# Five up blocks as seven products of quarters' sums, in a hybrid layer on one core

## The chip, the core and the metric

One Trainium2 chip, one of its cores. The metric is the device time of one execution in microseconds, from its start to its end; the median of the runs is quoted, and beside it one execution that the hardware profiler recorded. The engines have short names in the profile: PE is TensorE's matmuls, PEld its weight loads, DVE is VectorE, ACT is ScalarE, POOL is GpSimd, SP is SyncE, which issues most of the DMAs.

## What is computed

One layer over 512 tokens of width 1024 in float32. An mLSTM and a sparse attention with compressed, selected and window branches share one input product; their outputs go through `w_out`; then comes the feed-forward part with a causal convolution of width 3 on the gate, and a gated embedding with a last norm:

```python
x = x + jnp.concatenate([m_out, a_out], axis=-1) @ w_out[i]
x = x + conv_ffn(rms_norm(x, ln2_g[i]), w_up[i], conv_w[i], conv_b[i], w_down[i])
gate = jax.nn.sigmoid(rms_norm(x, ple_norm_g[i]) @ w_ple_gate[i])
x = x + gate * (p[i].astype(x.dtype) @ w_ple_proj[i])
return rms_norm(x, final_g)

def conv_ffn(h, w_up, conv_w, conv_b, w_down):
    u = h @ w_up                                # 1024 -> 2 * 2048
    gate, val = jnp.split(u, 2, axis=-1)
    gate = lax.conv_general_dilated(gate, conv_w[:, None, :], ...) + conv_b
    return (jax.nn.silu(gate) * val) @ w_down   # 2048 -> 1024
```

## The kernel before

Features lie on the partitions and tokens along the free axis, so a product takes a block of 128 x 128 weights as the stationary operand and 512 tokens as the moving one. Every float32 operand is split into a high part, rounded to the type fp32r, and a low part, the rest; a product is then three matmuls per block of the contraction: high x high, high x low, low x high. The function `gemm` (L445) sends the 16 matmuls with the high weights first (L449, L450), then the 8 with the low weights (L453).

The weights come as a stream of jobs (`Stream`, L182), each of 512 KB, 128 x 1024 columns: `load` (L152) issues its DMA on SP into one of two rooms `raw`, `split` (L163) makes the high part on ACT (L166) and the low part on DVE (L167), each in one of two rooms. `step` (L214) starts a job's matmuls and splits the job behind it (`prepare(1)`, L221). Other work is hung on the kernel's own count of time with `st.after`. Each engine works through its instructions in an order that is fixed when the program is built; the engines meet at semaphores.

In the feed-forward part the loop of L1203 makes 16 blocks f of two up jobs each: part 0 is the gate's 128 columns and part 1 the value's. `up_job` (L1105) multiplies `x2h` and `x2l`, the split of X x ln2_g without the norm's factor, by the weights. `up_evac` (L1150) takes the sum out of PSUM: for the gate a product with the norm's factor `n2["rb"]` on DVE (L1154), the convolution with one scaled copy on ACT (L1157) and two steps on DVE (L1158, L1159), and silu on ACT (L1160); for the value two products on DVE (L1164, L1165) and its split into `U` (ACT L1167, DVE L1168). POOL only clears the two columns in front of the gate (L1153). The PSUM banks are taken from two pairs in turn (`pW`, L106). The norm's factor comes from `start_norm` (L1123) soon after the first up jobs. Then 16 down jobs follow (`down_job`, L1184), and the last pass, in which the last tile's matmuls have 256 columns (L1333 to L1335).

POOL's other large work lies in the attention, far ahead: the scaling of the exponentials (L810).

Of the kernel before, what the change touches and what calls it, by code (L numbers as in the profile page):

```python
# [15 lines left out]
S = 512  # L16
PE_ORDER = False
D = 1024
KB = 8
# [23 lines left out]
LASTW = 256  # L43
SPLIT = 384
# [29 lines left out]
def hybrid_block_kernel(ctx: ExitStack, tc: tile.TileContext, a, out):  # L74
# [88 lines left out]
    def split(name, raw, shape):  # L163
        hi = wpool.tile(shape, F32R, tag="hi", name=name + "h")
        lo = wpool.tile(shape, F32R, tag="lo", name=name + "l")
# [16 lines left out]
    class Stream:  # L182


        def __init__(self):
            self.jobs, self.loaded, self.ready, self.cur, self.done = [], [], [], None, set()
            self.now, self.events, self.debt = 0.0, [], 0.0

        def add(self, name, src, shape, run):
            self.jobs.append((name, src, shape, run))  # L190

        def load(self, depth):
            while len(self.loaded) < depth and self.jobs:
                name, src, shape, run = self.jobs.pop(0)
                self.loaded.append((name, load(name, src, shape), shape, run))
                if name == "mv3":
                    early[0] = None

        def prepare(self, depth):
            while len(self.ready) < depth and (self.jobs or self.loaded):  # L200
                self.load(1)
                name, raw, shape, run = self.loaded.pop(0)
                self.ready.append((name, run, split(name, raw, shape)))
# [58 lines left out]
    identb = consts.tile([128, 128], BF, name="identb")  # L262
    maskt = consts.tile([128, 128], BF, name="maskt")
# [204 lines left out]
    gz = consts.tile([128, NT, 36], F32, name="gz")  # L468
    sg = consts.tile([128, NT, 24], F32, name="sg")
# [130 lines left out]
    VW = 4 * 132  # L600

    def vones(j, h):
        return vo[:, j * VW + h * 132:j * VW + h * 132 + 130]

# [518 lines left out]
    def start_norm(norm, acc, name):  # L1123
# [9 lines left out]
        def rows(ah, al):  # L1133
# [12 lines left out]
            for fn in norm.get("pending", []):  # L1146
                fn()
        st.after(T_NS, stats)

    def up_evac(f, part, ps, rb2):  # L1150
        if part == 0:
            zg = fpool.tile([128, S + 2], F32, name=f"zg{f}", tag="zg")
            GE.memset(zg[:, 0:2], 0.0)  # L1153
            VE.tensor_mul(zg[:, 2:S + 2], ps, rb2)  # L1154
            cw = lambda j: cols[:, C_CW + 16 * j + f:C_CW + 16 * j + f + 1]
            cv = fpool.tile([128, S], F32, name=f"cv{f}", tag="cv")
            SE.activation(cv, zg[:, 2:S + 2], AF.Identity, scale=cw(2), bias=cols[:, C_CB + f:C_CB + f + 1])  # L1157
            VE.scalar_tensor_tensor(cv, zg[:, 1:S + 1], cw(1), cv, op0=ALU.mult, op1=ALU.add)  # L1158
            VE.scalar_tensor_tensor(cv, zg[:, 0:S], cw(0), cv, op0=ALU.mult, op1=ALU.add)  # L1159
            SE.activation(cv, cv, AF.Silu)  # L1160
            n2["cv"] = cv
        else:
            zv = fpool.tile([128, S], F32, name=f"zv{f}", tag="zv")
            VE.tensor_mul(zv, ps, rb2)  # L1164
# [38 lines left out]
    for f in range(16):  # L1203
        for part in range(2):
# [19 lines left out]
    gF = main.tile([128, 2, 512], F32, tag="mixa", name="gF")  # L1224
# [218 lines left out]
```

## Time and profile before

| | us |
|---|---|
| median of three runs (626.46 to 627.56) | 626.55 |
| the profiled execution | 627.01 |
| its span, from the first to the last instruction | 625.2 |
| PE busy in the span | 613.9 |
| DVE busy | 417.8 |
| ACT busy | 317.8 |
| POOL busy | 62.2 |

The page gives busy time by engine and by 40 equal slices of the span; the other views group instructions by line, list them in order of time, or sum them over a stretch. A matmul's duration in these rows holds its way through the array; how densely matmuls follow each other is read from their starts.

### The profile page before, as it was taken

To read this page: it belongs to the slowest core of one execution; us is meant where nothing else is said; L and a number is where in the kernel's file an instruction comes from. 1 tells how busy PE (TensorE), PEld (TensorE's weight loads), DVE (VectorE), ACT (ScalarE), POOL (GpSimd) and SP (SyncE) were. 2 spreads that over 40 slices of the span, in tenths; PEclk is the share of its full clock that TensorE was granted. 3 is DMA by queue.
4 is the path that set the end of the run, shared out by engine and by line. 5 is a ranking of instruction groups with operands and counts; after the bars stand their busy time and mean duration, and the time that the engine had idled before them with its cause. 6 is when DMAs were issued, how large, how long until landed. Compare 5 with 4: busy or idle time off the path is not lost. (4 is left out here: it accounts for less than half of the span.)

```text
span 625.2 us, 8416 instructions
## 1 busy us (share of the span) xinstructions
PE 613.9 (98%) x3011; PEld 500.0 (80%) x3011; DVE 417.8 (67%) x800; ACT 317.8 (51%) x665; POOL 62.2 (10%) x132
## 2 busy tenths in 40 slices
PE   9999999999999999999999999999999999999994
PEld 7888877777777777888878888888888888888884
DVE  6988857787777878882977565655556434345386
ACT  7456556677667766653745333334334223233254
POOL 0400009332333400000000000000000000000000
PEclk9999999999999999999999999999999999999998
DMA  8812136112221323122233332233333222634703
GB/s 315 297 63 73 34 102 156 48 35 68 68 65 38 110 93 101 35 69 67 95 108 101 102 97 83 91 100 101 102 101 102 94 94 84 166 103 142 195 1 136
DMA packets 23210, 63.04 MB, mean 101 GB/s; under 512 B 2744, under 2 KB 7736, under 8 KB 23100
## 3 DMA queue, kind: packets, MB, share of 16 engines
q1 hardware_dynamic: 21632, 59.93, 29.5%
q0 software_dynamic: 1248, 2.16, 1.5%
q8 instruction: 24, 0.39, 0.3%
q10 hardware_dynamic: 288, 0.41, 0.2%
q14 instruction: 18, 0.15, 0.1%
HBM read 56.72 MB, written 2.10 MB: 94 GB/s over the span
## 5 line engine op out<-in xcount | busy, mean ns | idle before, releaser
L810 POOL TENSOR_SCALAR E<-E,rr,sg 128x512 f32<-128x512 f32 (+3 forms) x54 | 38.0, 704 | 72.0 <-DVE rr L805 57.8
L839 DVE TENSOR_TENSOR pl<-pt,ph 128x512 fp32r<-128x512 f32 x40 | 27.2, 686 | 7.3 <-ACT ph L838 6.9
L1164 DVE TENSOR_TENSOR zv<-pu,n2rb 128x512 f32<-128x512 f32 x16 | 11.0, 690 | 31.1 <-PE pu L453 31.1
L1167 ACT ACTIVATE u<-zv 128x512 fp32r<-128x512 f32 x16 | 10.1, 632 | 42.6 <-DVE zv L1165 42.6
L838 ACT ACTIVATE ph<-pt 128x512 fp32r<-128x512 f32 x40 | 23.7, 599 | 15.4 <-PE pt L835 14.0
L835 PE MATMUL pt<-cols,E 128*128 128x128 f32 x160 | 26.4, 274 | 0.5 <-DVE E L810 0.4
L1154 DVE TENSOR_TENSOR zg<-pu,n2rb 128x512 f32<-128x512 f32 x16 | 11.1, 692 | 22.3 <-PE pu L453 22.3
L1153 POOL MEMSET zg<- 128x2 f32 x16 | 1.5, 100 | 242.2 <-DVE cv L1159 149.7
L835 PEld LDWEIGHTS pt<-cols,E 128*128 128x128 f32 x160 | 19.9, 140 | 6.4 <-DVE E L810 1.1
L1194 DVE TENSOR_TENSOR X<-pd,X 128x512 f32<-128x512 f32 x8 | 5.5, 692 | 29.2 <-PE pd L453 29.2
L1157 ACT ACTIVATE cv<-zg,cols 128x512 f32<-128x512 f32 x16 | 13.1, 817 | 20.8 <-DVE zg L1154 20.8
L1160 ACT ACTIVATE cv<-cv 128x512 f32<-128x512 f32 x16 | 10.1, 632 | 25.8 <-DVE cv L1159 25.8
L803 ACT ACTIVATE E<-s,nm 128x384 f32<-128x384 f32 (+2 forms) x48 | 22.2, 471 | 0.0
L843 PE MATMUL pv<-ph,V 128*128 128x512 f32 x40 | 18.8, 471 | 0.0
L1168 DVE TENSOR_TENSOR u<-zv,u 128x512 fp32r<-128x512 f32 x16 | 11.0, 691 | 9.8 <-ACT u L1167 9.8
L805 DVE RECIPROCAL rr<-rs 128x3 f32<-128x3 f32 x32 | 5.5, 172 | 16.8 <-ACT E L803 16.7
L845 PE MATMUL pv<-pl,V 128*128 128x512 f32 x40 | 16.5, 411 | 0.1
L793 DVE TENSOR_REDUCE nm<-s 128x2 f32<-128x768 f32 (+2 forms) x24 | 16.3, 680 | 0.0
L286 DVE TENSOR_TENSOR acc<-acc,sq 128x512 f32<-128x512 f32 x21 | 14.4, 684 | 0.1
L803 ACT ACTIVATE Ec<-s,nm 128x32 f32<-128x32 f32 x24 | 6.8, 283 | 13.5 <-DVE nm L793 10.5
L1159 DVE SCALAR_TENSOR_TENSOR cv<-zg,cols,cv 128x512 f32<-128x512 f32 x16 | 12.0, 751 | 0.5
L1158 DVE SCALAR_TENSOR_TENSOR cv<-zg,cols,cv 128x512 f32<-128x512 f32 x16 | 11.9, 746 | 0.0
(1219 smaller groups left out, 2023.3 us busy)
## 6 DMA issues: line engine op xcount, KB each, us to landing
X<-in_xg SPq DMA_DIRECT2D x1, 2048.0 KB, 8.7
xo<-xturn SPq DMA_DIRECT2D x32, 64.0 KB, 2.1
wgr<-in_w_pg SPq DMA_DIRECT2D x4, 512.0 KB, 4.0
s1r<-in_w_s SPq DMA_DIRECT2D x3, 676.0 KB, 8.9
xT<-in_xg SPq DMA_DIRECT2D x3, 514.0 KB, 7.9
rawx<-in_w_mv SPq DMA_DIRECT2D x3, 512.0 KB, 6.7
Q<-hlq POOLq DMA_DIRECT2D x12, 128.0 KB, 3.1
out_y<-xo SPq DMA_DIRECT2D x3, 512.0 KB, 2.6
```

The lines of the kernel that those rows point to most:

```text
L286: return VE.tensor_add(acc[:, :n], acc[:, :n], sq[:, :n])
L793: VE.tensor_reduce(out=nm[:, 1:3], in_=sw, axis=AX.X, op=ALU.max, negate=True)
L803: SE.activation(e, p, AF.Exp, bias=nm[:, b:b + 1], accum_out=rs[:, b:b + 1])
L810: eng.tensor_scalar(e, e, rr[:, b:b + 1], sg[:, i, 3 * h + b:3 * h + b + 1], op0=ALU.mult, op1=ALU.mult)
L835: TE.transpose(pt[:, r * 128:(r + 1) * 128], Es[r][:, c0:c0 + 128], ident)
L838: SE.activation(ph, pt, AF.Copy)
L839: VE.tensor_sub(pl, pt, f32(ph))
L843: TE.matmul(pv, vs, ph, start=first, stop=False)
L845: TE.matmul(pv, vs, pl, start=False, stop=last)
L1157: SE.activation(cv, zg[:, 2:S + 2], AF.Identity, scale=cw(2), bias=cols[:, C_CB + f:C_CB + f + 1])
L1158: VE.scalar_tensor_tensor(cv, zg[:, 1:S + 1], cw(1), cv, op0=ALU.mult, op1=ALU.add)
L1159: VE.scalar_tensor_tensor(cv, zg[:, 0:S], cw(0), cv, op0=ALU.mult, op1=ALU.add)
```

## The change

Blocks f = 7 to 11 are computed as a 2 x 2 product of halves with seven products in place of eight. The contraction (8 blocks of 128) is cut in two halves, the tokens in two halves of 256, and the two columns of the product are gate and value. The left factors are quarters of the weights and sums of them, the right ones quarters of the normed input and sums of those. Each product has 4 blocks of contraction, three matmuls each, of 256 columns (`seven`). A block's stream entries are four: the gate's weights (products 1 and 2), the first two weights' sums (6 and 5), the other two (7 and 3; the input of product 3 is a plain quarter), and half of the value's weights (product 4). The value's weights are loaded with the second entry and the last two load nothing; POOL makes the four sums s1 to s4 when that load is entered (`landed_b`), in three rooms of 128 x 1024 columns of which a block takes two. The products stand in halves of four PSUM banks, with the other four for the next block, and are put together by seven additions on DVE and one copy on ACT.

For this the input is scaled by the norm's factor beforehand (`scaled_input`, in eight rounds), split into `xnh` and `xnl`; POOL makes 16 sums of its quarters in `Tf`, which are split in four rounds (`split_sums`). From f = 5 on the ordinary blocks read `xnh` and `xnl` too and lose the factor `rb` in their evacuation: the gate's sum is copied by ACT, the value's has one product on DVE in place of two.

Rooms: `raw`, `hi` and `lo` get a third room while `st.ahead` is set (from f = 6 to f = 11), the stream splits two jobs ahead and loads three. `identb`, `maskt`, `gz` and `sg` move to a pool that ends with the attention, the rows of `vo` become 130 columns a head in place of 132, and the room for descriptors of DMAs issued by POOL becomes 1024 bytes. `U`'s quarters, `xo`, `x3h` and `gF` change places.

```diff
+FAST = (7, 8, 9, 10, 11)
+UNSCALED = 5
+T_XN = 0.4, 5.4
+T_TS = 2.0, 5.4
+AHEAD = 3
...
+    turns = {}
+    def more(tag, n, extra, shape, dt, name):
+        if st.ahead:
+            turns[tag] = (turns.get(tag, -1) + 1) % (n + extra)
+            if turns[tag] >= n:
+                return fpool.tile(shape, dt, tag=tag, bufs=extra, name=name)
+        return wpool.tile(shape, dt, tag=tag, bufs=n, name=name)
...
-            raw = wpool.tile(shape, F32, tag="raw", bufs=2, name=name + "r")
+            raw = more("raw", 2, 1, shape, F32, name + "r")
-        hi = wpool.tile(shape, F32R, tag="hi", name=name + "h")
+        hi = more("hi", 2, 1, shape, F32R, name + "h")
+        lo = more("lo", 2, 1, shape, F32R, name + "l")
...
-                self.prepare(1)
+                self.prepare(self.depth)
+                self.load(self.ahead)
...
-    gz = consts.tile([128, NT, 36], F32, name="gz")
-    sg = consts.tile([128, NT, 24], F32, name="sg")
+    identb = apool.tile([128, 128], BF, name="identb")
+    maskt = apool.tile([128, 128], BF, name="maskt")
+    gz = apool.tile([128, NT, 36], F32, name="gz")
+    sg = apool.tile([128, NT, 24], F32, name="sg")
...
-    VW = 4 * 132
+    VW = 4 * 130
...
+            elif f < UNSCALED:
+                yield from gemm(ps, wh, wl, range(KB), x2h, x2l, range(KB))
             else:
-                yield from gemm(ps, wh, wl, range(KB), x2h, x2l, range(KB))
+                yield from gemm(ps, wh, wl, range(KB), xnh, xnl, range(KB))
+                up_evac(f, part, ps, None)
+                return
...
+            for q, b in enumerate((0, 4, 1, 5, 2, 6, 3, 7)):
+                st.after(T_XN[0] + T_XN[1] * q, lambda b=b: scaled_input(b))
...
+            if rb2 is None:
+                SE.activation(zg[:, 2:S + 2], ps, AF.Copy)
...
+            if rb2 is None:
+                VE.tensor_mul(zv, ps, n2["cv"])
...
+    def scaled_input(b):
+        xn = t2k(f"xn{b}")
+        i = VE.scalar_tensor_tensor(xn, X[:, b], cols[:, C_G2 + b:C_G2 + b + 1], n2["rb"], op0=ALU.mult, op1=ALU.mult)
+        SE.activation(xnh[:, b], xn, AF.Copy)
+        VE.tensor_sub(xnl[:, b], xn, f32(xnh[:, b]))
+        n2["xn", b] = xn
+        if b >= 4:
+            j = b - 4
+            top = n2["xn", j]
+            b11, b12, b21, b22 = top[:, 0:H], top[:, H:], xn[:, 0:H], xn[:, H:]
+            t1, t2, t3, t4 = (Tf[:, j, q] for q in range(4))
+            GE.tensor_sub(t1, b12, b11)
+            GE.tensor_sub(t3, b22, b12)
+            GE.tensor_sub(t2, b22, t1)
+            GE.tensor_sub(t4, b21, t2)
+    def split_sums(j):
+        SE.activation(Th[:, j], Tf[:, j], AF.Copy)
+        VE.tensor_sub(Tl[j // 2][:, j % 2], Tf[:, j], f32(Th[:, j]))
+    def seven(ps, w, x):
+        (wh, wl), (rh, rl) = w, x
+        for j in range(4):
+            TE.matmul(ps, wh[:, j], rh(j), start=j == 0, stop=False)
+            TE.matmul(ps, wh[:, j], rl(j), start=False, stop=False)
+            yield 0.24
+        for j in range(4):
+            TE.matmul(ps, wl[:, j], rh(j), start=False, stop=j == 3)
+            yield 0.12
...
+    def fast_banks(f):
+        fast_turn[0] += 1
+        if fast_turn[0] % 2:
+            ps = [pG(f"pfa{f}"), pT(f"pfb{f}"), pG(f"pfc{f}"), pT(f"pfd{f}")]
+        else:
+            sa = pSa(f"pfa{f}")
+            ps = [sa[:, 0], sa[:, 1], pSb(f"pfc{f}"), pV(f"pfd{f}")]
+        return [p[:, t0:t0 + H] for p in ps for t0 in (0, H)]
...
+        def landed_b(raw):
+            r0, d["r1"] = d["r0"], raw
+            if not rooms:
+                rooms.append(fpool.tile([128, 3, 8, 128], F32, bufs=1, name="ws", tag="xturn"))
+                rooms.append(0)
+            sums = []
+            for _ in range(2):
+                sums.append(rooms[0][:, rooms[1] % 3])
+                rooms[1] += 1
+            s2, s1, s3, s4 = sums[0][:, 0:4], sums[0][:, 4:8], sums[1][:, 0:4], sums[1][:, 4:8]
+            GE.tensor_add(s1, raw[:, 0:4], raw[:, 4:8])
+            GE.tensor_sub(s2, s1, r0[:, 0:4])
+            GE.tensor_sub(s3, r0[:, 0:4], raw[:, 0:4])
+            GE.tensor_sub(s4, r0[:, 4:8], s2)
+            d["sums"] = sums
+        def prep_b(name, raw, shape):
+            return split(name, d["sums"][0], shape)
+        def prep_c(name, raw, shape):
+            return split(name, d["sums"][1], shape)
+        def prep_d(name, raw, shape):
+            return split(name, d["r1"][:, 4:8], shape)
+        def run_a(wh, wl):
+            d["ps"] = fast_banks(f)
+            d["u"] = t2k(f"fu{f}")
+            d["v"] = t2k(f"fv{f}")
+            p1, p2 = d["ps"][0:2]
+            yield from seven(p1, half((wh, wl), 0), quarter(0, 0))
+            v1 = d["v"][:, H:]
+            yield from seven(p2, half((wh, wl), 1), quarter(4, 0))
+            SE.activation(v1, p1, AF.Copy)
+            d["zg"] = gate_rows(f)
+            VE.tensor_add(d["zg"][:, 2:2 + H], p2, v1)
+        def run_b(wh, wl):
+            p1, p2, p6, p5 = d["ps"][0:4]
+            u2, u4 = d["u"][:, 0:H], d["v"][:, 0:H]
+            yield from seven(p6, half((wh, wl), 0), tsum(1))
+            yield from seven(p5, half((wh, wl), 1), tsum(0))
+            VE.tensor_add(u2, p6, d["v"][:, H:])
+            VE.tensor_add(u4, p5, u2)
+        def run_c(wh, wl):
+            p5, p7, p3 = d["ps"][3:6]
+            u2, u3, u4 = d["u"][:, 0:H], d["u"][:, H:], d["v"][:, 0:H]
+            d["zv"] = fpool.tile([128, S], F32, name=f"zv{f}", tag="zv")
+            yield from seven(p7, half((wh, wl), 0), tsum(2))
+            yield from seven(p3, half((wh, wl), 1), quarter(4, H))
+            VE.tensor_add(d["zg"][:, 2 + H:], p3, u4)
+            convolve(f, d["zg"])
+            VE.tensor_add(u3, p7, u2)
+            VE.tensor_add(d["zv"][:, H:], p5, u3)
+        def run_d(wh, wl):
+            zv, p4 = d["zv"], d["ps"][6]
+            yield from seven(p4, (wh, wl), tsum(3))
+            VE.tensor_add(zv[:, 0:H], p4, d["u"][:, H:])
             VE.tensor_mul(zv, zv, n2["cv"])
-            uh, ul = U[f // 4][:, 0, f % 4], U[f // 4][:, 1, f % 4]
-            SE.activation(uh, zv, AF.Copy)
-            VE.tensor_sub(ul, zv, f32(uh))
+            hidden(f, zv)
...
+        st.add(f"wu{f}0", a["w_up"][:, f, 0], full, run_a, landed=landed_a)
+        st.add(f"wu{f}s", a["w_up"][:, f, 1], full, run_b, prep_b, landed_b)
+        st.add(f"wu{f}t", None, full, run_c, prep_c)
+        st.add(f"wu{f}1", None, [128, 4, 128], run_d, prep_d)
...
+    xnh = main.tile([128, KB, S], F32R, tag="mixa", name="xnh")
+    xnl = fpool.tile([128, KB, S], F32R, bufs=1, tag="xo", name="xnl")
+    Tf = main.tile([128, 4, 4, H], F32, tag="B16", bufs=3, name="tf")
...
+    st.until(f"wu{UNSCALED - 1}1")
+    Th = main.tile([128, 4, 4, H], F32R, tag="XH", name="th")
+    Tl = [main.tile([128, 2, 4, H], F32R, tag=f"XL{h}", name=f"tl{h}") for h in range(2)]
+    for j in range(4):
+        st.after(T_TS[0] + T_TS[1] * j, lambda j=j: split_sums(j))
+    st.until(f"wu{min(FAST) - 2}1")
+    st.depth, st.ahead = 2, AHEAD
+    st.until("wu71")
+    U.append(main.tile([128, 2, 4, S], F32R, tag="B16", bufs=3, name="u2"))
+    st.until("wu111")
+    U.append(main.tile([128, 2, 4, S], F32R, tag="XH", name="u3"))
+    st.depth, st.ahead = 1, 0
...
-    nc = _bacc.Bacc("TRN2", target_bir_lowering=False, num_devices=1)
+    nc = _bacc.Bacc("TRN2", target_bir_lowering=False, num_devices=1, dynamic_dma_scratch_size=1024)
```

## Rows read from the trace of the kernel before

**Rows 1.** The page: busy us, share, count of instructions; TensorE clock in 40 slices.

```profile
PE 613.9 (98%) x3011; PEld 500.0 (80%) x3011; DVE 417.8 (67%) x800; ACT 317.8 (51%) x665; POOL 62.2 (10%) x132
...
PEclk9999999999999999999999999999999999999998
```

**Rows 2.** Windows, blocks 7 to 11: length; busy of PE, PEld, DVE, ACT, POOL; clock.

```profile
386.92:441.32 54.40, 54.40 (x242) 45.07 (x240) 31.78 (x40) 20.47 (x25) 0.50 (x5) 1.00 0.30 97
```

**Rows 3.** Timeline of PE, block 7: start, duration, engine, line, operands, shape, count.

```profile
386.92 0.39 PE L449 MATMUL pu<-x2h,wu70h 128*128 128x512 f32 x1
...
390.55 1.98 PE L453 MATMUL pu<-x2h,wu70l 128*128 128x512 f32 x8
392.36 0.39 PE L449 MATMUL pu<-x2h,wu71h 128*128 128x512 f32 x1
...
397.80 0.39 PE L449 MATMUL pu<-x2h,wu80h 128*128 128x512 f32 x1
```

**Rows 4.** Timeline of PE in the last pass.

```profile
614.82 0.28 PE L1334 MATMUL pg1last<-wres,x3la 128*128 128x256 f32 x1
614.94 0.28 PE L1335 MATMUL pg1last<-wres,x3h 128*128 128x256 f32 x1
```

**Rows 5.** Groups by line, blocks 7 to 11: busy us, mean ns, idle before and releaser.

```profile
L1157 ACT ACTIVATE cv<-zg,cols 128x512 f32<-128x512 f32 x5 | 4.1, 818 | 7.2 <-DVE zg L1154 7.2
L1167 ACT ACTIVATE u<-zv 128x512 fp32r<-128x512 f32 x5 | 3.2, 632 | 15.0 <-DVE zv L1165 15.0
L166 ACT ACTIVATE wu90h<-wu90r 128x1024 fp32r<-128x1024 f32 x1 | 1.1, 1062 | 0.6 <-PE pu L450 0.6
...
L1159 DVE SCALAR_TENSOR_TENSOR cv<-zg,cols,cv 128x512 f32<-128x512 f32 x5 | 3.8, 752 | 0.2
L1168 DVE TENSOR_TENSOR u<-zv,u 128x512 fp32r<-128x512 f32 x5 | 3.5, 692 | 3.5 <-ACT u L1167 3.5
...
L167 DVE TENSOR_TENSOR wu71l<-wu71r,wu71h 128x1024 fp32r<-128x1024 f32 x1 | 1.2, 1218 | 0.0
```

**Rows 6.** Groups by line of DVE, whole span: a sum of 256 columns out of PSUM.

```profile
L852 DVE TENSOR_TENSOR ao<-pv,os 64x256 f32<-64x256 f32 x16 | 6.7, 416 | 1.4 <-ACT os L849 1.2
```

**Rows 7.** Timeline of DVE in block 12, with the idle time before and its releaser.

```profile
446.96 0.69 DVE L1154 TENSOR_TENSOR zg<-pu,n2rb 128x512 f32<-128x512 f32 x1 [1.63 <-PE pu L453]
447.57 1.22 DVE L167 TENSOR_TENSOR wu130l<-wu130r,wu130h 128x1024 fp32r<-128x1024 f32 x1
```

**Rows 8.** Timeline of POOL in the attention: 32 and 512 columns, one input.

```profile
213.17 0.37 POOL L810 TENSOR_SCALAR Ec<-Ec,rr,sg 128x32 f32<-128x32 f32 x1
213.51 0.77 POOL L810 TENSOR_SCALAR E<-E,rr,sg 128x512 f32<-128x512 f32 x1
```

**Rows 9.** Timeline of DVE and POOL in the attention, around 211.

```profile
210.35 1.22 DVE L167 TENSOR_TENSOR mq7l<-mq7r,mq7h 128x1024 fp32r<-128x1024 f32 x1
210.42 1.79 POOL L810 TENSOR_SCALAR E<-E,rr,sg 128x512 f32<-128x512 f32 x1
...
212.32 0.69 DVE L839 TENSOR_TENSOR pl<-pt,ph 128x512 fp32r<-128x512 f32 x1
...
212.42 0.77 POOL L810 TENSOR_SCALAR E<-E,rr,sg 128x512 f32<-128x512 f32 x1 [0.21 <-DVE rr L805]
```

**Rows 10.** Timeline of DVE and POOL in the attention, around 95.

```profile
94.37 1.48 DVE L477 TENSOR_TENSOR hlq<-zq,hlq 128x512 fp32r<-128x512 f32 x1
...
94.54 0.76 POOL L810 TENSOR_SCALAR E<-E,rr,sg 128x512 f32<-128x512 f32 x1
```

**Rows 11.** Loads of L160 from 384 to 442: issue to landing.

```profile
DMA to landing us min/median/max: 3.2/3.3/4.1
```

**Rows 12.** Instructions of one raw tile: durations in ns, first and last start.

```profile
L167 DVE TENSOR_TENSOR wu70l<-wu70r,wu70h x1: 1215/1215/1215, 382.3 to 382.3; 128x1024 fp32r<-128x1024 f32 x1
```

**Rows 13.** Timeline of PE in the first up jobs.

```profile
315.76 0.39 PE L441 MATMUL pu<-x2h,wu01h 128*128 128x512 f32 x1
316.00 0.40 PE L442 MATMUL pu<-x2la,wu01h 128*128 128x512 f32 x1
```

More of the change, by code (lines that the diff above doesn't have):

```diff
@@ L186, in __init__, with add @@
             self.jobs, self.loaded, self.ready, self.cur, self.done = [], [], [], None, set()
-            self.now, self.events, self.debt = 0.0, [], 0.0
-        def add(self, name, src, shape, run):
-            self.jobs.append((name, src, shape, run))
+            self.now, self.events, self.debt, self.depth, self.ahead = 0.0, [], 0.0, 1, 0
+        def add(self, name, src, shape, run, prep=split, landed=None):
+            self.jobs.append((name, src, shape, run, prep, landed))
         def load(self, depth):
             while len(self.loaded) < depth and self.jobs:
-                name, src, shape, run = self.jobs.pop(0)
-                self.loaded.append((name, load(name, src, shape), shape, run))
+                name, src, shape, run, prep, landed = self.jobs.pop(0)
+                raw = load(name, src, shape) if src is not None else None
+                if landed:
+                    landed(raw)
+                self.loaded.append((name, raw, shape, run, prep))
                 if name == "mv3":
@@ L201, in prepare @@
                 self.load(1)
-                name, raw, shape, run = self.loaded.pop(0)
-                self.ready.append((name, run, split(name, raw, shape)))
+                name, raw, shape, run, prep = self.loaded.pop(0)
+                self.ready.append((name, run, prep(name, raw, shape)))
         def after(self, us, fn):
@@ L1147, in rows, with gate_rows, convolve @@
                 fn()
+            for q, b in enumerate((0, 4, 1, 5, 2, 6, 3, 7)):
+                st.after(T_XN[0] + T_XN[1] * q, lambda b=b: scaled_input(b))
         st.after(T_NS, stats)
+    def gate_rows(f):
+        zg = fpool.tile([128, S + 2], F32, name=f"zg{f}", tag="zg")
+        GE.memset(zg[:, 0:2], 0.0)
+        return zg
+    def convolve(f, zg):
+        cw = lambda j: cols[:, C_CW + 16 * j + f:C_CW + 16 * j + f + 1]
+        cv = fpool.tile([128, S], F32, name=f"cv{f}", tag="cv")
+        SE.activation(cv, zg[:, 2:S + 2], AF.Identity, scale=cw(2), bias=cols[:, C_CB + f:C_CB + f + 1])
+        VE.scalar_tensor_tensor(cv, zg[:, 1:S + 1], cw(1), cv, op0=ALU.mult, op1=ALU.add)
+        VE.scalar_tensor_tensor(cv, zg[:, 0:S], cw(0), cv, op0=ALU.mult, op1=ALU.add)
+        SE.activation(cv, cv, AF.Silu)
+        n2["cv"] = cv
@@ L1150, in up_evac, with hidden @@
+    def hidden(f, zv):
+        uh, ul = U[f // 4][:, 0, f % 4], U[f // 4][:, 1, f % 4]
+        SE.activation(uh, zv, AF.Copy)
+        VE.tensor_sub(ul, zv, f32(uh))
     def up_evac(f, part, ps, rb2):
         if part == 0:
[L1152 to L1161, printed above, removed]
+            zg = gate_rows(f)
+            if rb2 is None:
+                SE.activation(zg[:, 2:S + 2], ps, AF.Copy)
+            else:
+                VE.tensor_mul(zg[:, 2:S + 2], ps, rb2)
@@ new lines, in quarter, with tsum @@
+    def quarter(k0, t0):
+        return (lambda j: xnh[:, k0 + j, t0:t0 + H]), (lambda j: xnl[:, k0 + j, t0:t0 + H])
+    def tsum(q):
+        return (lambda j: Th[:, j, q]), (lambda j: Tl[j // 2][:, j % 2, q])
+    fast_turn, rooms = [0], []
+    def fast_banks(f):
+        fast_turn[0] += 1
+        if fast_turn[0] % 2:
+            ps = [pG(f"pfa{f}"), pT(f"pfb{f}"), pG(f"pfc{f}"), pT(f"pfd{f}")]
+        else:
+            sa = pSa(f"pfa{f}")
+            ps = [sa[:, 0], sa[:, 1], pSb(f"pfc{f}"), pV(f"pfd{f}")]
+        return [p[:, t0:t0 + H] for p in ps for t0 in (0, H)]
@@ new lines, in up_fast, with landed_a @@
+    def up_fast(f):
+        d = {}
+        half = lambda w, q: (w[0][:, 4 * q:4 * q + 4], w[1][:, 4 * q:4 * q + 4])
+        def landed_a(raw):
+            d["r0"] = raw
+        def landed_b(raw):
[51 more added lines that the diff above has]
+            VE.tensor_add(zv[:, 0:H], p4, d["u"][:, H:])
+            VE.tensor_mul(zv, zv, n2["cv"])
+            hidden(f, zv)
+        full = [128, KB, 128]
+        st.add(f"wu{f}0", a["w_up"][:, f, 0], full, run_a, landed=landed_a)
+        st.add(f"wu{f}s", a["w_up"][:, f, 1], full, run_b, prep_b, landed_b)
+        st.add(f"wu{f}t", None, full, run_c, prep_c)
+        st.add(f"wu{f}1", None, [128, 4, 128], run_d, prep_d)
```

26 lines of the change are left out of this document (14 added, 12 removed).

## The prediction

> **What bounds the kernel now.** [...] The windows view then shows the stage that is changed: five up blocks, f = 7 to 11, take 54.40 us, PE is busy for all of it, VectorE for 31.78, POOL for half a microsecond [rows 2]. No wait ends last there except TensorE's own queue. The timeline of PE gives the pace: job wu70 starts at 386.92, wu71 at 392.36, wu80 at 397.80 [rows 3], so a block of two jobs is 10.88 us for 48 matmuls of 512 columns, 0.2267 us from start to start.
>
> **The change, part by part.**
>
> *The seven products (gain).* A fast block has 7 products of 12 matmuls of 256 columns, 84 in place of 48 of 512. Matmuls of 256 columns, each with weights of its own, run in the last pass 0.12 us from start to start [rows 4]: not half of 0.2267 but 0.0067 more. 84 x 0.12 = 10.08 us, so a block saves 0.80 us and not the eighth (1.36) that the count of products suggests. Five blocks: 4.0 us. This lies on the path as long as the operands are there in time.
>
> *ScalarE.* A fast block asks for three copies of 1024 columns at 1.06, a half one and three of 512 or fewer at 0.63 at most and one scaled copy at 0.82 [rows 5], together at most 6.6 us of 10.08. It binds nothing.
>
> *VectorE.* Three subtractions of 1024 columns at 1.22, one of 512 at about 0.69, seven sums of 256 columns out of PSUM at 0.42 [rows 6], two convolution steps at 0.75, the product and the last subtraction at 0.69 [rows 5]: 3.66 + 0.69 + 2.91 + 1.50 + 1.38 = 10.1 us in 16 instructions. An instruction here starts about 0.08 before the one ahead of it ends (the split starts at 447.57, the evacuation ahead of it ends at 446.96 + 0.69 = 447.65) [rows 7], so they need 8.8 us of 10.08. That fits alone, but without the slack of before (31.78 / 5 = 6.4 of 10.88).
>
> *POOL, the new member on the path.* Four sums of 512 columns a block. No two-input POOL instruction stands in the trace. The lower bound is the one-input one of 512 columns, 0.77; the upper is twice that, 1.54 [rows 8, 9]. The form with 32 columns takes 0.37, so a column costs (0.77 - 0.37) / 480 = 0.83 ns and the start 0.34; if the second input is read after the first, 0.34 + 2 x 0.43 = 1.2 us. I take 1.2.
>
> *The common port.* VectorE's split of mq7 started at 210.35 and POOL's scaling at 210.42: POOL's took 1.79 where the next of the same shape took 0.77 beside a VectorE instruction that read PSUM [rows 9]. The other way round, the subtraction at 94.37 took 1.48 with POOL's 0.76 in it [rows 10], 0.79 more than the 0.69 of its shape. So a VectorE instruction with two SBUF inputs and a POOL instruction go one after the other, and one that reads PSUM doesn't mind. The handover overlaps: 210.42 + 1.79 - 0.77 = 211.44, 0.13 before the split ended, and 94.37 + 1.48 - 0.69 = 95.16, 0.14 before POOL ended. Of VectorE's 10.1 us, eight instructions, 7.2 us, have two SBUF inputs: 7.2 - 8 x 0.11 = 6.3 us of port time. POOL's four: 4 x (1.2 - 0.15) = 4.2. Together 10.5 of 10.08 us.
>
> *The supply loop.* The raw half-pair of the next block goes into the room that this block's last sum sets free (three raw rooms, two loads a block). A load lands 3.3 us behind its issue [rows 11]; with the semaphores about 3.5 us in which POOL has nothing to do, which leaves it 6.6 of 10.08. If VectorE's port work moves into POOL's idle time as far as it can, 6.3 - 3.5 = 2.8 is left beside POOL's 4.2: 7.0, or 0.4 over. If it is spread evenly, 6.3 x 6.6 / 10.08 = 4.1 + 4.2 = 8.3, 1.7 over. I take 1.0 over for each turn, a little under the middle, since the seven sums out of PSUM (2.9 us) can stand beside POOL. There are four turns (sums of blocks 8 to 11). The first start with a lead: the second room's sums are ready some 3.5 + 1.1 + 6.6 + 2.3 (split) = 13.5 us behind a block's start and wanted 10.08 + 5.76 = 15.8 behind it, 2.3 spare. Loss: 4 x 1.0 - 2.3 = 1.7 us, late in the five blocks. While a split waits for sums, the convolution and the evacuations queued behind it on VectorE and ScalarE wait too, but their PSUM banks are wanted only two blocks later; who waits in the end is PE, for the low half of the next product.
>
> [...]
>
> *Edits at nothing.* The scaled input adds to f = 1 to 4 two rounds a block on VectorE (0.75 + 0.69 each), 2.9 us beside 6.4 of 10.88; a split there is done 7 us before its low matmuls (wu70l starts at 382.3 and takes 1.2, the matmuls that read it start at 390.55) [rows 3, 12], which hides it; without that cover PE would wait for what is over. POOL's 16 differences of 256 columns (4 x some 0.8 in 10.88 us) stand there too, with nothing waiting until f = 7. The four splits of the differences fall into f = 5 and 6, where each block has lost two multiplications on VectorE (1.4 us); the last is due 18.2 of the kernel's own microseconds behind wu41, 22 with its two copies, and wanted at 21.8 + 2.9 = 24.6. If that is late, PE waits once, 1 to 2 us at most. Loads: the same bytes; SP's queue holds the next gate half behind a val half that waits for its room, which the turn contains already. The memset of zg's two columns stands on POOL's queue among the sums and is small. The moved constants, the rows of 130 in place of 132 and the smaller descriptor room touch the attention stage alone; I set them at 0, with 0.5 us either way, since nothing there is in the changed stage.
>
> **Sum.** The profiled execution took 627.01 us (span 625.2 and 1.8 around it). -4.0 + 1.7 = -2.3 gives 624.7 there; the runs' median is 626.55, so 624.25. Rounded, with half of the 0.5 above against it, 624.5.
>
> **Rivals.**
>
> *The sums are hidden.* With POOL's sum near its lower bound, 4 x (0.77 - 0.15) = 2.5 and 2.8 to 4.1 of VectorE's stay within 6.6. Nothing is lost: 626.55 - 4.0 = 622.5. For it speaks that both port users are in queues that can shift by some microseconds; against it, that the second input has to be read as well.
>
> *The port is the bound, slower.* If the handover gives nothing back and the two add up in full, 7.2 + 4.8 = 12.0 us a block, and with a sum at 1.35 (between my value and the upper bound) 12.6: 2.5 over, 4 x 2.5 - 2.3 = 7.7 lost, 626.55 - 4.0 + 7.7 = 630.2. With 1.2 it would be 627.9. It decides from 1.6 us over per turn. For it speaks POOL's 1.79 and VectorE's 1.48 [rows 9, 10], and that VectorE's order is fixed ahead, so that an instruction that waits for the port holds those behind it. Against it speaks the measured overlap at both handovers. [...]
>
> *The narrow matmuls don't run at 0.12.* The row for 0.12 is from a pass in which VectorE and ScalarE do little. In the first up jobs, with both busy, 512-column matmuls came 0.24 apart (315.76 to 316.00) [rows 13], 0.013 over. On 84 x 5 matmuls that is 5.5 us, and the seven products would do nothing: 628.0 with all else hidden; at a third of it 624.4. Break-even is 10.88 / 84 = 0.1295 us. Against it: the blocks of before run at 0.2267 beside a VectorE that is busy 58% of the time [rows 2, 3].
>
> **How the numbers follow.** Forecast (sums partly late) 0.42, own range 623.0 to 625.9; hidden 0.25, around 622.5; port-bound 0.20, 627.7 to 632; pace 0.13, 624 to 628. The range 622.3 to 629.5 leaves out the upper half of the port case and little else. About 0.2% (1.25 us) is what a measurement of this kernel can tell from no change. Faster by more: 0.27 of the forecast, all of hidden, 0.03 of pace: 0.55. Within: 0.14, 0.03 of the port case, 0.07: 0.24. Slower: 0.01, 0.17, 0.03: 0.21.
>
> **What would show it.** Fast blocks that follow each other at 10.08 us, with spacing 0.12, show the gain; blocks 10 and 11 should be longer than 7 and 8, with PE waiting for a VectorE split, and the split for a sum. POOL's sums should show at about 1.2 alone and up to 2.4 with a split in them. If all five blocks are 10.08, the loss of 1.7 was wrong; if the spacing is over 0.1295, the first term was; if POOL alone is over 1.35, the port case holds. A PE wait ahead of f = 7's second job would show the differences late.

## The result, and the profile after

The changed kernel takes 631.51 us, median of six runs (630.69 to 633.34), against 626.65 for the kernel before (626.46 to 627.68): a ratio of 1.0073, interval 1.0062 to 1.0084. It is slower, by 4.9 us, where 624.5 was forecast, and lies above the range. The profiled execution took 630.95 us (span 629.2), 3.9 more than that of before and 0.6 under the median of its own kernel, so the account by stages has 4.0 us of span to place.

First the page of after: busy us, share and count of each engine, then the busy tenths of VectorE and POOL and the TensorE clock in 40 slices. They answer to [rows 1].

```profile
PE 613.5 (98%) x3191; PEld 505.6 (80%) x3191; DVE 458.4 (73%) x843; ACT 338.5 (54%) x698; POOL 119.6 (19%) x168
...
DVE  6988857787777778873979998999844434345476
...
POOL 0500009332333400000014514745000000000000
PEclk9999999999999999999999999999999999999998
```

PE's busy sum is nearly that of before (613.5 for 613.9), over a longer span. VectorE has 41 us more and POOL 57. The five blocks hold 22 and 30 of these; 21 and 25 lie in the blocks ahead of them, where the input is scaled and its sums are made, and there PE does not wait behind the first block (busy for all of the 65.29 us from 322.87 to 388.16). The clock is not the reason in this execution: its row is that of before, digit for digit.

The windows of after, one line for each of the blocks 7 to 11 (length; busy of PE, PEld, DVE, ACT, POOL; clock), answer to [rows 2]:

```profile
388.16:398.18 10.02, 10.02 (x86) 10.02 (x84) 8.99 (x11) 5.01 (x7) 6.63 (x5) 1.00 0.30 94
398.18:410.65 12.47, 10.68 (x87) 10.17 (x86) 12.26 (x15) 6.08 (x9) 8.21 (x6) 1.00 0.29 96
410.65:420.67 10.02, 10.02 (x86) 10.02 (x85) 10.02 (x14) 5.92 (x8) 6.41 (x5) 1.00 0.16 52
420.67:433.75 13.08, 10.58 (x86) 10.18 (x85) 12.87 (x18) 5.55 (x8) 7.41 (x6) 1.00 0.38 122
433.75:444.03 10.28, 10.26 (x86) 10.06 (x85) 9.53 (x15) 6.44 (x9) 1.85 (x2) 1.00 0.25 77
```

Three blocks run as the first term of the sum says, at 10.02 to 10.28 us; two take 12.5 and 13.1, and in those two VectorE is busy for nearly all of it. Together 55.87 us, where before had 54.40: 1.5 us more, though the products alone should have given 4.0.

The other 2.5 us lie where the prediction set the change at nothing. From the starts of the same jobs in the two traces (timeline of PE, first matmul of each job), after is late by 0.46 us at the first projection (42.87 for 42.41) and 0.62 at the first up job; by 1.23 at wu10; by 2.71 at wu120, which is the five blocks; by 4.07 at the first job behind the down stage; by 4.53 at the last rows; and it ends 4.0 late, the last 11 us being half a microsecond shorter. So five places: the start (+0.6), the first up block (+0.6), the five blocks (+1.5), the down stage and the pass behind it (+1.3 and +0.5), the tail (-0.5).

### The profile page after: what moved, and what is told of

It reads as the page before. It is cut to its first block, busy times and chain, and to the rows that moved or that the text cites. A ratio compares the mean times of both kernels' runs of the same rounds, so it can differ in the third digit from the quotient of the medians.

```text
span 629.2 us, 8908 instructions
## 1 busy us (share of the span) xinstructions
PE 613.5 (98%) x3191; PEld 505.6 (80%) x3191; DVE 458.4 (73%) x843; ACT 338.5 (54%) x698; POOL 119.6 (19%) x168
## 4 chain that ended last, share of the span: by engine, by line
PE 70%; DVE 20%; issue 5%; ACT 3%; DMA 1%; POOL 0%; DVEq 0%; ACTq 0%; POOLq 0%
PE pd L466 5%; PE pd L470 5%; PE pd L467 5%; PE pt L854 2%; PE pu L467 2%; PE pu L466 2%; PE pu L470 2%; PE ptm L413 2%; PE pmq L470 2%; PE pc L417 2%; PE pmq L466 2%; PE pv L862 2%; PE pmq L467 2%; PE pv L864 1%; PE mo L1055 1%
## 5 line engine op out<-in xcount | busy, mean ns | idle before, releaser
L500 POOL DMA_DIRECT2D Q<-hlq x12 | 6.3, 541 | 54.9 <-ACT hlq L495 54.9
L1192 DVE TENSOR_TENSOR u<-zv,u 128x512 fp32r<-128x512 f32 x16 | 16.2, 1015 | 0.4 <-ACT u L1191 0.4
L1184 DVE SCALAR_TENSOR_TENSOR cv<-zg,cols,cv 128x512 f32<-128x512 f32 x16 | 13.0, 810 | 1.7 <-ACT cv L1183 1.7
L1185 DVE SCALAR_TENSOR_TENSOR cv<-zg,cols,cv 128x512 f32<-128x512 f32 x16 | 12.4, 774 | 0.2
L1055 PE MATMUL mo<-vo,mw 128*128 128x130 f32 x80 | 11.8, 279 | 0.0
```

The costliest lines, as they stand in the source:

```text
L1055: TE.matmul(po[:, 0:130], Ws[j][:, (i - j) * 128:(i - j + 1) * 128], vones(j, h), start=(j == 0), stop=(j == i))
```

## Experiments

**One bank tile or VectorE.** In blocks 8 and 10 the order of PE's products is another than in 7, 9 and 11: the two halves of one two-bank tile hold products 1, 2 and 6, 5, and PE stands until VectorE has read the first half. PE's waits of after from 398 to 434 (who waits, for whom, us in total, times, longest):

```profile
PE pfa L1244 <- DVE wu100l L182: 1.4, 1, 1.4
PE pfd L1240 <- ACT wu81h L181: 1.1, 1, 1.1
PE pfc L1244 <- DVE wu10tl L182: 1.1, 1, 1.1
PE pfa L1240 <- DVE zg L1306: 0.7, 1, 0.7
```

The last is that tile; the others are low halves, or a copy, that come late. My first theory was that the tile, by the order it forces, is the loss.

```diff
-            ps = [sa[:, 0], sa[:, 1], pSb(f"pfc{f}"), pV(f"pfd{f}")]
+            ps = [sa[:, 0], pSb(f"pfc{f}"), pV(f"pfd{f}"), sa[:, 1]]
```

> One line of the changed kernel differs: in the even fast blocks (8 and 10) the first pair of products and the second pair no longer lie in the two halves of one two-bank PSUM tile; the banks go (first half of that tile, a single bank, another single bank, second half). In the trace of the changed kernel TensorE runs blocks 7, 9, 11 in 10.0 to 10.3 us and blocks 8 and 10 in 12.5 and 13.1; in those two it takes the products in another order and stands until VectorE has read the first half of the tile. Theory A (the shared tile): both blocks fall to 10.0 to 10.5 us, the five to 50.4 to 51.5 (from 55.87), the kernel to 626.5 to 627.5 us. Rival B (VectorE, stretched by GpSimd's sums, is full anyway and the tile only decides where it shows): blocks 8 and 10 give back under 1 us each or the other blocks grow, and the kernel stays at 629.5 to 631.

Measured: 632.82 us, ratio 1.0093 (1.0078 to 1.0109), above both forecasts. PE's order was now the written one in all five blocks, and block 8 took 10.00; but 9, 10 and 11 took 12.79, 12.79 and 11.70, the five 57.30. Theory A fell: the tile decides where the loss shows. Why the five blocks took 1.4 us more in the written order than in after (57.30 and 55.87) is open.

**The address of the rooms.** Shortening the value tile's rows from 132 to 130 columns made each of the three largest rooms (tag B16: u1, u2 and the last pass's weights among others) 128 bytes shorter. By the addresses in the two programs, all operands of the feed-forward part lay alike modulo 256 bytes before; after, u1, u2 and wres lie 128 bytes off the weights. In the trace of after, 512-column matmuls on u0 come 226.7 ns apart and on u3 227.9, those on u1 and u2 232.6 and 233.3.

```diff
-    vo = main.tile([128, NT * VW + 4 * S], F32, tag="B16", bufs=3, name="vo")
+    vo = main.tile([128, NT * VW + 4 * S + 32], F32, tag="B16", bufs=3, name="vo")
```

> One line differs: the tile that sets the size of the three large rooms gets 128 more bytes in each partition, so that all three rooms start at the same address modulo 256 bytes as the weights (in the changed kernel two of the three lie 128 bytes off it; in the kernel before none did). Theory A (address class): the 192 matmuls of the down stage that read the second and third quarter of the hidden rows go from 232.6 to 226.7 ns, 192 x 6 = 1.2 us, the 72 of the last pass on the two first weight halves from 233.2 to 226.6, 0.5 us: the kernel at 629.6 to 630.0 us. Rival B (the spacing comes from something else in these stages): no change, 631.3 to 631.7.

The other way round, the kernel before with this part of the change alone:

```diff
-    VW = 4 * 132
+    VW = 4 * 130
...
-        return vo[:, j * VW + h * 132:j * VW + h * 132 + 130]
+        return vo[:, j * VW + h * 130:j * VW + (h + 1) * 130]
```

> The kernel before with one part of the change alone: the rows of the value tile 130 columns apart instead of 132, which makes each of the three large rooms 128 bytes shorter and puts two of them 128 bytes off the weights' address modulo 256. Theory A (address class): the down stage 87.0 to 88.3 us, the last pass 0.5 more, 628.2 to 628.6 us. Rival: no change, 626.5 to 627.0.

One line of the windows view for the first down block of each, after, after with the 128 bytes, and before with the short rows, in this order:

```profile
487.58:498.63 11.05, 11.05 (x50) 9.01 (x48) 3.65 (x4) 2.40 (x3) 0.00 (x0) 1.00 0.30 96
```

```profile
492.28:503.16 10.88, 10.88 (x50) 9.01 (x49) 3.65 (x4) 2.40 (x3) 0.00 (x0) 1.00 0.31 98
```

```profile
484.79:495.84 11.05, 11.05 (x50) 9.01 (x48) 4.34 (x5) 2.35 (x3) 0.00 (x0) 1.00 0.29 96
```

0.17 us a block comes and goes with the 128 bytes, on a PE that is busy throughout. Eight blocks and 72 matmuls of the last pass: the second kernel lost nothing against before from wu130 to the last rows (7.44 us late and 7.46), the third 1.8 (628.67 us, ratio 1.0030, 1.0019 to 1.0040). Theory A holds for these stages in both directions. The whole time of the second kernel, 633.41 us (1.0086 to 1.0113), stayed out of the forecast: its five blocks took 60.5, with 17.7 in block 10. Windows of 2 us inside that block, with the granted clock as the last but two figures:

```profile
427.00:429.00 2.00, 0.46 (x4) 0.26 (x3) 2.00 (x2) 0.63 (x1) 2.00 (x2) 1.00 0.00 0
...
431.00:433.00 2.00, 1.38 (x7) 1.32 (x7) 2.00 (x4) 0.63 (x1) 1.96 (x3) 0.50 0.00 0
...
435.00:437.00 2.00, 2.00 (x12) 2.00 (x11) 0.00 (x0) 0.59 (x1) 0.00 (x0) 0.50 0.29 117
437.00:439.00 2.00, 2.00 (x18) 2.00 (x18) 1.75 (x3) 1.65 (x3) 0.00 (x0) 0.96 0.00 0
```

PE had stood 1.5 us at 422 and 2.1 at 427 when the granted clock fell to 0.50, from 430.3 to 437.2, with matmuls 0.21 apart instead of 0.12: 25 of them, so some 2.4 us beside the waits. That the stalls brought the fall about is not shown.

**Both edits.**

> Both edits at once, the banks of the even blocks and the 128 bytes. If the two losses are independent and as large as theory A says for each (4.4 and 1.7 us): 625.0 to 626.0 us, under the kernel before by some 1 us. If rival B holds for the banks: 628 to 629.5.

Measured: 631.56 us (1.0059 to 1.0085), above both forecasts. The address part gave its 1.8 (5.12 us late at wu130 and at the last rows); the blocks took 57.46. This is the kernel in which the loss can be read best, since PE's order is plain and the clock 1.00:

```profile
388.96:398.97 10.01, 10.01 (x85) 10.01 (x84) 8.98 (x11) 5.02 (x7) 6.73 (x5) 1.00 0.29 92
398.97:408.98 10.01, 10.01 (x87) 10.01 (x86) 10.01 (x12) 4.98 (x8) 6.45 (x6) 1.00 0.24 74
408.98:421.88 12.90, 10.75 (x86) 10.14 (x85) 12.80 (x16) 6.46 (x9) 8.27 (x5) 1.00 0.22 77
421.88:434.67 12.79, 10.91 (x87) 10.25 (x86) 12.69 (x16) 5.71 (x9) 7.08 (x6) 1.00 0.26 83
434.67:446.42 11.75, 10.23 (x87) 10.04 (x86) 11.65 (x19) 5.96 (x9) 0.65 (x3) 1.00 0.39 121
```

Blocks 7 and 8 use up a lead; from 9 on a block lasts as long as VectorE works on it, 12.8 us. Its timeline there, VectorE, POOL and one load's issue (start, duration, engine, line, operands):

```profile
407.11 1.74 POOL L1282 TENSOR_TENSOR ws<-ws,wu90r 128x512 f32<-128x512 f32 x1
...
407.62 1.78 DVE L1192 TENSOR_TENSOR u<-zv,u 128x512 fp32r<-128x512 f32 x1
...
408.93 1.61 POOL L1284 TENSOR_TENSOR ws<-wu90r,ws 128x512 f32<-128x512 f32 x1
...
409.66 1.97 DVE L182 TENSOR_TENSOR wu90l<-wu90r,wu90h 128x1024 fp32r<-128x1024 f32 x1
...
411.69 0.33 SPq L175 DMA_DIRECT2D wu10sr<-in_w_up  x1
...
415.09 1.68 POOL L1281 TENSOR_TENSOR ws<-wu10sr 128x512 f32<-128x512 f32 x1 [4.55 <-DMA wu10sr<-in_w_up]
...
415.86 1.99 DVE L182 TENSOR_TENSOR wu9tl<-ws,wu9th 128x1024 fp32r<-128x1024 f32 x1
...
417.77 1.77 DVE L1331 TENSOR_TENSOR zv<-zv,cv 128x512 f32<-128x512 f32 x1
...
419.80 1.45 DVE L182 TENSOR_TENSOR wu91l<-wu9sr,wu91h 128x512 fp32r<-128x512 f32 x1
...
421.17 1.77 DVE L1192 TENSOR_TENSOR u<-zv,u 128x512 fp32r<-128x512 f32 x1
```

The subtraction began at 407.62 and ended at 409.40, 0.55 behind the end of POOL's sum (407.11 + 1.74 = 408.85): it did its 0.69 when the sum was through, but for 0.14. The next sum took 1.61 in place of the 1.30 that one takes alone. In the next turn POOL's four sums (415.09 to 422.40) met two splits, the product and the subtraction: 1.99, 1.77, 1.45 and 1.77 us, where the same shapes take 1.22, 0.69, 0.68 and 0.69 alone (from 441.44 on in the same trace, POOL idle), together 3.7 more. Of VectorE's seven sums out of PSUM, which took 0.41 us beside a POOL sum (at 419.46) and 0.42 without one (at 443.17), four stood in the 4.55 us in which POOL had nothing. And the load that POOL waits for there was issued at 411.69, right behind VectorE's split of wu90 (409.66 + 1.97 = 411.63), which sets its room free, and not behind POOL's last sum (410.54): VectorE's lateness delays the loads too. VectorE itself waits for nothing in blocks 9 and 10.

**The sums taken away.**

```diff
+            if f > min(FAST):
+                d["sums"] = once
+                return
+            sums = once
```

> The kernel with both edits (banks and 128 bytes: 631.56 us, its five blocks 10.01, 10.01, 12.90, 12.79 and 11.75 us, VectorE busy 56.1 of their 57.5 us), but the weights' sums are formed for block 7 alone; blocks 8 to 11 split block 7's sums again, so 16 of the 20 additions on GpSimd are left out and the values of these blocks are not the network's. Theory C (VectorE is the bound, because its operations with two operands in SBUF take 1.8 instead of 0.7 us while GpSimd adds): VectorE's operations fall back to 0.69 and 1.22, all five blocks take 10.0 to 10.4 us, 50.2 to 51.5 together, and the kernel 624.8 to 626.0 us. Rival D (VectorE's own work of a block is over 10.08 us even alone): blocks 9 to 11 stay at 10.5 or more, the five at 52.5 or more, the kernel over 626.6. Rival E (the loads come late, not the sums): no gain, 630 or more.

Measured: 624.10 us, ratio 0.9956 (0.9943 to 0.9968), a little under theory C's forecast. The five blocks, in windows:

```profile
388.82:398.83 10.01, 10.01 (x85) 10.01 (x84) 8.12 (x14) 5.66 (x9) 0.10 (x1) 1.00 0.42 135
398.83:408.83 10.00, 10.00 (x86) 10.00 (x85) 9.10 (x16) 5.75 (x9) 0.10 (x1) 1.00 0.34 112
408.83:418.86 10.03, 10.03 (x86) 10.03 (x85) 9.17 (x16) 5.85 (x9) 0.10 (x1) 1.00 0.32 102
418.86:428.89 10.03, 10.03 (x87) 10.03 (x85) 9.13 (x16) 5.84 (x9) 0.10 (x1) 1.00 0.34 110
428.89:438.89 10.00, 10.00 (x87) 10.00 (x85) 9.11 (x16) 5.82 (x9) 0.10 (x1) 1.00 0.33 108
```

50.07 us, no wait. VectorE's own work is 9.1 us a block, so rival D falls, and POOL's sums added 12.8 - 9.1 = 3.7 to it. But this kernel frees the load rooms earlier too, so rival E is not yet out. Hence a kernel in which sums and loads stay and VectorE has one operation less:

```diff
-            hidden(f, zv)
+            SE.activation(U[f // 4][:, 0, f % 4], zv, AF.Copy)
+            SE.activation(U[f // 4][:, 1, f % 4], zv, AF.Copy)
```

> The kernel with both edits, but in the five blocks ScalarE copies the hidden row into the room of its low part and VectorE's subtraction (1.78 us under GpSimd's sums, 0.69 alone) is left out: the low part of these hidden rows is not the network's. GpSimd's sums and all loads stay. Theory C (VectorE is the bound): each of the blocks 9, 10 and 11 loses some 1.1 to 1.8 us, the five take 52.5 to 54.5 instead of 57.5 and the kernel 627 to 629 us. Rival E (the loads and the sums are the bound): within 1 us of 631.6.

Measured: 626.32 us (0.9984 to 1.0002 of before), the blocks 10.02, 10.00, 10.63, 11.02 and 10.82. The gain was 5.2, more than the 2.6 to 4.6 forecast, and 5.0 of it came in the five blocks. With the same loads and sums, E falls: VectorE's queue is the bound. Blocks 9, 10 and 11 lost 2.3, 1.8 and 0.9 us, 1.7 on average for an operation that took 1.78.

**Less of it: three blocks.** 

```diff
-FAST = (7, 8, 9, 10, 11)
+FAST = (7, 9, 11)
...
-            turns[tag] = (turns.get(tag, -1) + 1) % (n + extra)
+            turns[tag] = (turns.get(tag, 0 if tag == "raw" else -1) + 1) % (n + extra)
```

> The kernel with both edits, with seven products in blocks 7, 9 and 11 only, an ordinary block between them, and the third load room used one job earlier, so that block 7's first weight sum can no longer run beside the split of block 0 (there it cost 0.6 us). Theory C (VectorE's backlog is what costs): a fast block's 12.8 us of VectorE and an ordinary block's 6.4 are 19.2 of the 20.96 us that TensorE needs for the two, so TensorE never waits: 3 x 10.02 + 2 x 10.88 = 51.8 us for the five, and against the kernel with no fast block (630.2) 1.8 less for the addresses and 2.6 less for the blocks: 625.3 to 626.3 us, under the kernel before. Rival E (late loads): fast blocks over 10.5, 627 or more.

Measured: 625.84 us, ratio 0.9984 (0.9975 to 0.9993). Behind the first it is as theory C had it: fast blocks 10.71, 10.02 and 10.02, and PE busy without a gap from block 8 on. The ordinary blocks took 11.05 instead of 10.88: their split weights stand, in turn, in the third room, 64 bytes off the others modulo 256. That the time came out as forecast is in part luck: the five took 52.86 where the sum had 51.8, but the first projection came 1.1 us earlier than in the kernel with no fast block (42.48 and 43.56).

The second line of the edit answers for the first up block. The timeline of after there:

```profile
314.24 1.29 POOL L1281 TENSOR_TENSOR ws<-wu7sr 128x512 f32<-128x512 f32 x1 [3.34 <-DMA wu7sr<-in_w_up]
...
314.67 1.94 DVE L182 TENSOR_TENSOR wu01l<-wu01r,wu01h 128x1024 fp32r<-128x1024 f32 x1
```

Block 7's first weight sum ran 66 us ahead of its use, since its load room was free; block 0's split took 1.94 us beside it, not 1.22, and PE waited. Without that sum there, wu10 started as late as wu00 (0.40 and 0.42 us), where after has 1.23 and 0.62. But the edit only moves the loss: all four sums of block 7 now stand right ahead of it, from 380.0 on, PE waits for the low half of wu70, and the block takes 10.71 instead of 10.02.

**No fast block.** 

```diff
-FAST = (7, 8, 9, 10, 11)
+FAST = ()
```

> No block in seven products: all sixteen up blocks run as before, the rest of the change stays (the layout, the input scaled once, the differences of the input's quarters, the deeper preparation). Theory A (the five blocks cost 1.5 us more than before, 55.87 against 54.40, and the first weight sum, which is drawn forward to 314 us, costs 0.6 by stretching a split; the rest is the layout): 629.2 to 629.8 us, some 2.8 us over the kernel before. Rival B (all of the loss comes with the seven products): 626.3 to 627.0.

Measured: 630.18 us (1.0040 to 1.0065): 3.4 us over the kernel before without a single product of quarters. It is 0.4 above the forecast; its blocks 7 to 11 took 54.96 instead of 54.40, and the three jobs among their ten that read weights in the third room took 0.15 to 0.19 more. So not all of the 3.4 stands in after in the same way: there the first projection was 0.46 late, here 1.16.

**The product in PSUM.** If only operations with two operands in SBUF are held, two of 512 columns can be freed with nothing left out: the value row and product stay in the bank of the last product.

```diff
-            zv, p4 = d["zv"], d["ps"][6]
+            zv, p4, p5 = d["ps"][8], d["ps"][6], d["ps"][3]
...
+            VE.tensor_add(zv[:, H:], p5, d["u"][:, H:])
```

> All five blocks in seven products, with both edits (banks and 128 bytes), the third load room used one job earlier as in the kernel with alternating blocks, and one more edit that leaves nothing out: the value row, its product with the convolved gate and what is split from it stay in the PSUM bank of the last product instead of an SBUF room. The number and shape of VectorE's operations is the same; two of 512 columns in each block now read one operand in SBUF instead of two. Theory C (only VectorE operations with two operands in SBUF are stretched by GpSimd's additions): both fall from 1.78 to 0.69 us, VectorE's 12.8 us per block to 10.6, blocks 9 to 11 to 10.1 to 10.8, the five to 50.5 to 52.0, the kernel to 623.6 to 625.2 us, under the kernel before. Rival F (any VectorE operation that touches SBUF is stretched, or the stretch moves whole to the splits): the two stay at 1.5 or more or the splits take it up, blocks 9 to 11 over 12 us, the kernel at 629 or more.

Measured: 625.38 us, ratio 0.9970 (0.9959 to 0.9981). The same subtraction under a POOL sum:

```profile
406.01 1.74 POOL L1283 TENSOR_TENSOR ws<-wu90r,wu9sr 128x512 f32<-128x512 f32 x1
...
406.51 0.68 DVE L1192 TENSOR_TENSOR u<-pfd,u 128x512 fp32r<-128x512 f32 x1
...
411.11 1.33 DVE L182 TENSOR_TENSOR wu9sl<-ws,wu9sh 128x1024 fp32r<-128x1024 f32 x1 [1.08 <-ACT wu9sh L181]
```

0.68 us, and VectorE is idle again, waiting 1.08 for a copy that waits for the sums. The five took 52.30 (10.65, 10.00, 10.23, 10.77, 10.65), a little over the forecast: in block 7 by the third room used earlier, as in the kernel with three blocks, and behind it by the supply loop, the next that is late.

**The start.** This kernel began its first projection at 43.59, 1.2 us behind the kernel before. POOL's and VectorE's rows of it, with the fill of the keys' room and the norm's first step of 4 columns:

```profile
25.18 1.86 POOL L743 MEMSET K<- 64x2112 f32 x1
25.21 1.86 DVE L312 TENSOR_SCALAR n1t<-n1v 128x4 int32<-128x4 int32 x1
```

The same in the kernel before, and then in after:

```profile
23.80 1.85 POOL L724 MEMSET K<- 64x2112 f32 x1
...
25.74 0.53 DVE L295 TENSOR_SCALAR n1t<-n1v 128x4 int32<-128x4 int32 x1
```

```profile
24.52 1.86 POOL L743 MEMSET K<- 64x2112 f32 x1
...
25.52 0.89 DVE L312 TENSOR_SCALAR n1t<-n1v 128x4 int32<-128x4 int32 x1
```

In the changed kernels the step ends with the fill (at 27.07 and 27.04 in this kernel, 26.41 and 26.38 in after). In the traces of all changed kernels but the one with the fill first, the fill starts anywhere from 24.06 to 25.41, and the first projection stands 18.3 to 18.4 us behind it (18.6 before); so a single trace gives this loss only to about half a microsecond. The fill is late because two small tables ahead of it on POOL's queue moved into the attention's rooms, free at 21.7 to 22.3, while they were written at 20.7 before. Two kernels and a repeat:

```diff
-    GE.tensor_copy(maskt, cols[:, C_MASK:C_MASK + 128])
-    GE.tensor_copy(identb, ident)
+    GE.memset(f32(K[64:128, :, 1, :]), 0.0)
...
+    GE.tensor_copy(maskt, cols[:, C_MASK:C_MASK + 128])
+    GE.tensor_copy(identb, ident)
```

> The kernel with the products in PSUM (625.38 us), with GpSimd's seven preparing operations at 22 to 27 us in another order: the large fill of the keys' room (1.86 us) first, the two small tables behind it instead of ahead. In the changed kernels these tables lie in the room that the attention frees at 22.3 us, in the kernel before in a room of their own, so there they were written at 20.7 and the fill ran 23.80 to 25.65; in this kernel it ran 25.18 to 27.04, and VectorE's first step of the first norm, 4 columns, took 1.86 us instead of 0.53 beside it. Theory G (the fill, now later, holds VectorE's small steps of the norm): that step takes 0.6 or less, the first projection starts at 42.3 to 42.8 us instead of 43.59, the kernel at 623.9 to 624.8 us. Rival H (the late start comes from the first loads or from code, not the fill): start at 43.3 or later, 625.2 to 625.7 us.

> The kernel before with one part of the change alone: the two small tables and the gates' two rooms lie in the attention's pool instead of the constants'. Theory G: the tables can be written only when that pool's rooms come free at some 22 us, GpSimd's large fill ends 0.7 to 1.4 us later than in the kernel before, and VectorE's norm step stretches with it: the first projection at 42.8 to 43.8 us instead of 42.41, the kernel at 627.0 to 628.1 us. Rival H: 626.4 to 627.0.

> The kernel with the products in PSUM again, beside the one with the fill first on the same chip: 625.0 to 625.7 us, the first projection at 43.3 to 43.8 us.

Measured: 623.83 us with the fill first, ratio 0.9950 (0.9938 to 0.9963), first projection at 41.59; 628.21 us for the rooms alone (1.0009 to 1.0027), first projection at 43.20; 625.42 us and 43.12 for the repeat. With the fill first:

```profile
22.11 1.86 POOL L737 MEMSET K<- 64x2112 f32 x1 [1.67 <-DVE lo L407]
...
24.86 0.17 DVE L312 TENSOR_SCALAR n1t<-n1v 128x4 int32<-128x4 int32 x1
```

Theory G holds, in both directions, with more than it forecast: the start came 0.7 ahead of its 42.3 to 42.8, and the rooms alone end 0.1 over 628.1. The kernel with the fill first leaves nothing out and is, by the medians, 3.0 us under the kernel before and 7.7 under the changed one. Some 0.8 of the 3.0 is the start (41.59 against 42.41), which the fill first might give the kernel before as well; that was not run. For the rooms alone the medians say 1.4 us (0.6 to 1.7) and the trace 0.8; the difference is open.

## Why the prediction was wrong

*The seven products:* right. Matmuls of 256 columns came 0.12 apart, and an unhindered block took 10.00 to 10.03 us against 10.08. The rival of slow narrow matmuls is out. *ScalarE:* right, 5.0 to 6.5 us a block. *VectorE alone:* 8.8 forecast, 9.1 measured; the working lists 15 instructions and counts 16, which by its own rule makes 8.9. *The sum on POOL:* 1.2 forecast, 1.30 measured alone (at 410.06 in the kernel with the products in PSUM, VectorE idle for the first 1.05 of it). *The common port:* what was read in [rows 9, 10] came again at 407.62, the subtraction and the sum one after the other with some 0.14 of overlap. A shared port is the prediction's reading of this; the traces show the order and the times, not the cause.

*The supply loop:* the step that failed. I let VectorE's reads of PSUM, 2.9 us, stand beside POOL's sums, and its port work fill POOL's idle time, and so took 1.0 us over per turn. The trace has it the other way: while POOL waits 4.5 us for its load, VectorE does four of its seven PSUM sums, and when POOL's four sums run, they meet two splits, the product and the subtraction, one each. VectorE's order is fixed in the program, so an instruction that is held delays all behind it: 9.1 + 3.7 = 12.8 us, 2.8 over per turn, not 1.0. The room that I took to be set free by the last sum was, once VectorE was late, set free by VectorE's split. That 7 and 8 run free came true in the kernel with plain bank order, but the lead was mis-sized too: 57.46 - 50.07 = 7.4 us lost there are four turns of 2.8 less 3.8, not 2.3. In after itself the two-bank tile changed PE's order and spread the loss over two blocks; 55.87 - 50.07 = 5.8 us lost where 1.7 stood. The rival "the port is the bound" had VectorE held by the sums, as the traces show it, and nearly the time, 630.2, by a sum of all port work (12.6 us a block); I held the small overlap against it, which was the wrong argument, since order and not overlap decides. It deserved more than 0.20. That its time came so near is partly luck: it had 7.7 lost in the blocks where after lost 5.8, and nothing for the edits below. Its sign, a sum of over 1.35 alone, did not show (1.30), and the case held all the same.

*Edits at nothing:* the other step that failed, 0 with 0.5 either way where +2.5 was measured. "Nothing there is in the changed stage" was no reason: the rows of 130 columns moved rooms whose next users are u1, u2 and the last pass's weights, +1.8; the tables' room delays a fill that holds VectorE's norm, +0.5 in after (0.8 in the trace of that part alone); the third load room let the first sum run into block 0, +0.6. The start is the least certain of these, since it differs by a microsecond and more between traces. The half microsecond that the tail gained is not separated. Neither of the two steps alone would have put the time out of the range: -4.3 + 5.8 with no other cost is 628.1, and 1.7 lost with 2.5 of such costs 626.5. Together they make 627.01 - 4.3 + 5.8 + 2.5 = 631.0, the profiled execution's time.

## What to carry to other kernels

When work goes to POOL, don't add up the times of the instructions that held each other here: lay the two queues beside each other and count each VectorE instruction with two SBUF operands that a POOL instruction can meet as held for most of the POOL instruction (here 0.8 to 1.1 us of a sum of 1.30), with everything queued behind. An operand left in PSUM took the instruction out of that here (0.68 us beside a sum). And a tile that is moved or resized is an edit to whatever uses the room, or the rooms behind it, later: list those users, their addresses and the moment each room comes free before setting it at zero.

## What the runs showed of the hardware

Matmuls of 512 columns with new weights each came 226.7 ns apart when moving operand and weights start alike modulo 256 bytes, and 232.6 to 233.3 when 128 bytes apart; with 256 columns there was no such cost (118 to 119 for 120). Only distances of 0, 64 and 128 bytes occur in these runs. Why is open. A fill, which reads nothing, held a VectorE step of 4 columns with one SBUF operand for 1.86 us (0.17 in the kernel with the fill first). And in one execution the granted clock fell to 0.50 for 6.8 us behind two stalls of 1.5 and 2.1 us, and the matmuls there took some 2.4 us more beside the waits.
